# Feed forward's second layer in column blocks of 512, and local attention's probabilities normalised on ScalarE

## The chip, the cores and the metric

The kernel runs on one core of a Trainium2 chip. Its time is the device time of one execution in microseconds (us), here as the median of three runs; smaller is better. The core has five engines that run their own queues in order: TensorE (PE, with its weight loads shown apart as PEld), VectorE (DVE), ScalarE (ACT), GpSimd (POOL) and SyncE (SP), which issues most DMAs.

## The reference, cut to what matters

The program computes two transformer blocks on 512 tokens of width 1024, in float32. The change lies in the second block. Its local attention has eight heads of 64 (two groups of keys and values, four heads each), a window of 128, and a sink in the softmax's sum:

```
scores = where(mask, scores + bias, NEG_INF)
m = max(max(scores), sink)
e = exp(scores - m)
denom = sum(e) + exp(sink - m)
probs = e / denom
out = probs @ v
```

The feed forward is two matrix products, with 4096 hidden features, and a layer norm behind it:

```
ff = square(relu(h @ w_ff1)) @ w_ff2          # 512x1024 @ 1024x4096, then 512x4096 @ 4096x1024
h  = layer_norm(ALPHA * h + ff, ln2_g, ln2_b)
```

## The kernel before, in words

Matrix products keep float32's precision by splitting each operand into a rounded high part and a low part: `mm3` (L94 to L99) multiplies high by high, high by low and low by high into one PSUM bank. `wblock` loads a block of weights of 1 MB by SP's queue into one of two raw slots, and `wsplit` (L77 to L90) makes the high part on ScalarE (L88) and the low part on VectorE (L89), in two halves of 128x1024 each, into one of two high and two low slots. Tokens lie in four tiles of 128 (`NT` = 4).

**Local attention** is `swa_units(c, qT)`, run four times (rounds 0 to 3, c = 0 to 3), each time with two heads, one of each group g, and four blocks n of 128 queries. Each round is interleaved with another generator: round 0 with `u_units(1)` (projections for the pooling mixer), round 1 with `q_units(1)`, round 2 with `u_units(0)`, round 3 with `wo2A_units` (first half of the output projection). In a round, the scores of block n go through L1165 (PE), L1167 and L1169 (VectorE: bias, row maximum). `soft(n)` takes the exponentials on ScalarE with the sums of rows (L1184), adds the sink's term and inverts (L1186, L1187 on VectorE), and multiplies by the inverse on GpSimd (L1189). `mix(n)` transposes the probabilities on PE (L1197), copies them out of PSUM on VectorE for odd n (L1199) and on ScalarE for even n (L1201), and multiplies by the values on PE (L1205). `pool_group` beside it copies a projection on ScalarE (L1222), sums windows on VectorE (L1226, L1229, L1231 gives `dT`), multiplies on PE (L1234) and evicts on ScalarE (L1235) and VectorE (L1236).

**Feed forward** runs in two halves hf of 2048 hidden features. The first layer makes 16 slabs of 128 features by 512 tokens (`fh` and `fl`, high and low), each with 24 matmuls of 512 columns: weights are the stationary operand and the tokens move. In the second layer the slabs are stationary and the weights move: a column block of 256 outputs has four accumulators (one per token tile, two banks "mm" and two banks "sc"), filled from two weight blocks kg of 8 slabs each; `done(t)` adds an accumulator to x1 (L1421). The last column block of the second half runs tile by tile, so that the layer norm can follow.

The order in each engine's queue is set by a scheduler from the program's order and dependencies; a row that waits holds back all behind it on its engine.

Of the kernel before, what the change touches and what calls it, by code (L numbers as in the profile page):

```python
# [13 lines left out]
AF = mybir.ActivationFunctionType  # L14
ALU = mybir.AluOpType
# [13 lines left out]
def hybrid_moe_block(ctx: ExitStack, tc: tile.TileContext, A, out):  # L29
    nc = tc.nc  # L30
    V, P, T, G = nc.vector, nc.scalar, nc.tensor, nc.gpsimd
# [26 lines left out]
    def bank(tag, shape=(128, 512)):  # L58
        return psp.tile(list(shape), F32, name=f"ps_{tag}", tag=tag, bufs=NPS[tag])
# [32 lines left out]
    def wblock(parts, nk=8, n=256, **kw):  # L92
        return wsplit(wload(parts, nk, n), nk, n, **kw)

    def mm3(ps, lh, ll, rh, rl, first=True, last=True):

        seq = list(zip(lh, rh)) + list(zip(lh, rl)) + list(zip(ll, rh))
        for i, (a, b) in enumerate(seq):
            T.matmul(ps, a, b, start=first and i == 0, stop=last and i == len(seq) - 1)  # L99
# [807 lines left out]
    for t in range(NT):  # L907
# [21 lines left out]
                    op=ALU.is_equal)  # L929
# [227 lines left out]
    def swa_units(c, qT):  # L1157

        sc = pa.tile([128, NT, 2, 256], F32, name="sc")
        mx = small.tile([128, NT, 2], F32, name="wmx")  # L1160
        for n in range(NT):
            j0 = 0 if n else 128
            ps = bank("sc", (128, 2, 256))
            for g in range(2):
                T.matmul(ps[:, g, j0:], qT[:, n * 128:(n + 1) * 128], kT[g][:, (n - 1) * 128 + j0:(n + 1) * 128],  # L1165
                         start=True, stop=True)
            V.scalar_tensor_tensor(sc[:, n, :, j0:], ps[:, :, j0:], 0.125, bias[:, c, :, j0:],  # L1167
                                   op0=ALU.mult, op1=ALU.add)
            V.tensor_reduce(mx[:, n], sc[:, n, :, j0:], axis=AX.X, op=ALU.max)  # L1169
            yield  # L1170
        sk = sink[:, None, :, c].to_broadcast([128, NT, 2])
        V.tensor_tensor(mx, mx, sk, op=ALU.max)
        nm = small.tile([128, NT, 2], F32, name="wnm")
        V.tensor_scalar(nm, mx, -1.0, None, op0=ALU.mult)
        es_ = small.tile([128, NT, 2], F32, name="wes")
        V.tensor_tensor(es_, nm, sk, op=ALU.add)
        P.activation(es_, es_, AF.Exp)
        sm = small.tile([128, NT, 2], F32, name="wsm")
        rr = small.tile([128, NT, 2], F32, name="wrr")
        po = bank("po", (128, NT, 128))  # L1180
        def soft(n):
            j0 = 0 if n else 128
            for g in range(2):
                P.activation(sc[:, n, g, j0:], sc[:, n, g, j0:], AF.Exp, bias=nm[:, n, g:g + 1],  # L1184
                             accum_out=sm[:, n, g:g + 1])
            V.tensor_tensor(rr[:, n], sm[:, n], es_[:, n], op=ALU.add)  # L1186
            V.reciprocal(rr[:, n], rr[:, n])  # L1187
            scn = sc[:, n, :, j0:]
            G.tensor_tensor(scn, scn, rr[:, n, :, None].to_broadcast([128, 2, 256 - j0]), op=ALU.mult)  # L1189

        def mix(n):
            nj = 2 if n else 1
            pt = bank("pt", (128, 2, 2, 128))
            eT = pa.tile([128, 2, 2, 128], F32, name="eT")
            for g in range(2):
                for j in range(2 - nj, 2):
                    T.transpose(pt[:, g, j], sc[:, n, g, j * 128:(j + 1) * 128], ident)  # L1197
            if n % 2:
                V.tensor_copy(eT[:, :, 2 - nj:], pt[:, :, 2 - nj:])  # L1199
            else:  # L1200
                P.activation(eT[:, :, 2 - nj:], pt[:, :, 2 - nj:], AF.Copy)  # L1201
            for j in range(2 - nj, 2):
                for g in range(2):
                    gs = slice(64 * g, 64 * g + 64)
                    T.matmul(po[gs, n], vv[:, n - 1 + j, gs], eT[:, g, j], start=j == 2 - nj, stop=j == 1,  # L1205
                             skip_group_check=True)

        soft(0)
        yield
        for n in range(NT):  # L1210
            if n < NT - 1:
                soft(n + 1)
            mix(n)
            yield
        pof = po.rearrange("p a b -> p (a b)")
        P.activation(yTh[1][:, c], pof, AF.Copy)
        V.tensor_tensor(yTl[1][:, c], pof, yTh[1].bitcast(F32)[:, c], op=ALU.subtract)
        yield
# [79 lines left out]
    ALPHA = 2.0 ** 0.25  # L1298
# [51 lines left out]
    gr, br = row("ln1_g_2"), row("ln1_b_2")  # L1350
# [14 lines left out]

    w_ff1 = A["w_ff1_2"].rearrange("o (k p) n -> p (o k) n", p=128)
    w_pg = A["w_ple_gate_2"].rearrange("o (k p) n -> p (o k) n", p=128)
    w_ff2 = A["w_ff2_2"].rearrange("o (g k p) n -> p (o g) k n", p=128, k=8)
    es7.close()
    es8 = ExitStack()  # L1370
    pw = es8.enter_context(tc.tile_pool(name="pw", bufs=1, reuse_waits="tile"))
# [3 lines left out]
    for hf in range(2):  # L1375
        qs = [pf.tile([128, 4, S], F32R, name=f"fq{i}", bufs=1) for i in range(3)] + [quad(FR[6 + i]) for i in range(5)]
        fh = [qs[2 * (i // 4)][:, i % 4] for i in range(16)]
# [9 lines left out]
        for b in range(8):  # L1387
            c0 = 2048 * hf + 256 * b
# [13 lines left out]
                ff1_out(2 * b + c, feat3(w, 128 * c))  # L1402
        if hf == 1:
            gr, br = row("ln2_g_2"), row("ln2_b_2")
        for nb in range(4):
            cs = slice(256 * nb, 256 * nb + 256)
            last = hf == 1 and nb == 3
            pss = [bank("mm"), bank("mm"), bank("sc"), bank("sc")]
            ws = {}

            def ff2(t, kg):
                hi, lo = ws[kg]
                ts = slice(t * 128, (t + 1) * 128)
                mm3(pss[t][:, :256], [fh[8 * kg + k][:, ts] for k in range(8)], [fl[8 * kg + k][:, ts] for k in range(8)],
                    [hi[:, k, :256] for k in range(8)], [lo[:, k, :256] for k in range(8)],
                    first=kg == 0, last=kg == 1)

            def done(t):
                xs = x1[:, t, cs]
                if hf == 0:  # L1420
                    V.scalar_tensor_tensor(xs, xs, ALPHA, pss[t][:, :256], op0=ALU.mult, op1=ALU.add)  # L1421
                else:
                    V.scalar_tensor_tensor(xs, pss[t][:, :256], 1.0, xs, op0=ALU.mult, op1=ALU.add,
                                           accum_out=acc[:, t, nb:nb + 1])

            for kg in range(2):
                ws[kg] = wblock([(w_ff2[:, 2 * hf + kg, :, cs], 256)])
                if not last:
                    for t in range(NT):
                        ff2(t, kg)  # L1430
            if last:
                dst = [pw.tile([128, 2048], F32R, name=f"wg{i}") for i in range(2)]
                wg = {0: wblock([(w_pg[:, :, :256], 256)], dst=dst)}
            for t in range(NT):
                if last:
                    ff2(t, 0)
                    ff2(t, 1)
                done(t)
                if last:
                    layer_norm(t, gr, br, 4)  # L1440
                    if t > 1:
                        turn(x1[:, t - 2], t - 2, h_h, h_l)

# [50 lines left out]
```

## Time and profile before

| what | us |
|---|---|
| median of three runs | 1415.14 (1410.7 to 1417.24) |
| the profiled execution, its own time | 1417.58 |
| its span, first to last instruction | 1415.8 |
| TensorE busy | 1327.5 (94%) |
| VectorE, ScalarE, GpSimd busy | 633.8, 407.4, 54.5 |
| local attention with what runs beside it, and the output projection behind it | 870 to 1018 |
| second layer of feed forward, first half | 1085.43 to 1177.45 |
| second layer, second half, first three column blocks | 1267.39 to 1336.40 |

Times in the trace count from the span's start. In a row of the timeline the figures are start and length, then engine, line, operation, output<-input and the count of instructions merged; in brackets stands how long the engine sat idle before it and what released it. Lengths of matmuls include their drain, so a stretch's time is read from one start to the next.

### The profile page before, as it was taken

The page shows a single profiled execution, that of the slowest core. Times are in us where ns is not written, and L with a number is a line of the kernel's source. Part 1 is how long each engine was busy: PE and PEld are TensorE (multiplying, and loading weights), DVE is VectorE, ACT ScalarE, POOL GpSimd, SP SyncE. Part 2 cuts the span into 40 slices and gives each one's busy share as a digit, 9 for nine tenths or more (in the row PEclk, how much of TensorE's full clock was granted, in tenths as well). Part 3 has the DMA queues.
Part 4 walks back from the last instruction along what each step waited for, and adds up shares of the span by engine and source line. Part 5 has one row for each costly group of instructions (what it writes and reads, how often), then busy time and mean ns, then how long its engine had stood idle before and what let it go on. Part 6 is the DMA issues. An engine that isn't in the chain of part 4 may idle for free. (4 is left out here: it accounts for less than half of the span.)

```text
span 1415.8 us, 20242 instructions
## 1 busy us (share of the span) xinstructions
PE 1327.5 (94%) x8025; PEld 970.9 (69%) x8025; DVE 633.8 (45%) x1637; ACT 407.4 (29%) x809; POOL 54.5 (4%) x67
## 2 busy tenths in 40 slices
PE   8999999998998799999768989999999999999998
PEld 8878787885453344444213348677988998889998
DVE  7775538856432031314001145567743224442384
ACT  5445635432121010101001022533433113331231
POOL 0220200200000000000000000210000000000000
PEclk9999999998999999999999999999999999999999
DMA  5211231675789999998999971113322222332331
GB/s 184 91 30 61 58 106 54 212 282 199 306 322 391 419 418 421 418 392 333 413 420 420 420 266 60 52 39 119 119 89 90 90 90 90 95 106 96 122 109 57
DMA packets 107104, 285.11 MB, mean 201 GB/s; under 512 B 6275, under 2 KB 76505, under 8 KB 82430
## 3 DMA queue, kind: packets, MB, share of 16 engines
q1 hardware_dynamic: 101132, 272.85, 51.2%
q10 hardware_dynamic: 4754, 7.09, 1.5%
q0 software_dynamic: 1120, 3.84, 0.8%
q8 instruction: 64, 1.05, 0.3%
q14 instruction: 34, 0.28, 0.1%
HBM read 279.56 MB, written 4.20 MB: 200 GB/s over the span
## 5 line engine op out<-in xcount | busy, mean ns | idle before, releaser
L848 PE MATMUL ps_mm<-slot,xT 128*64 128x512 f32 (+1 forms) x1024 | 211.0, 615 | 28.7 <-DMA slot<-in_w_up_dram 18.8
L89 DVE TENSOR_TENSOR slot<-slot,slot 128x1024 fp32r<-128x1024 f32 (+2 forms) x118 | 141.0, 1210 | 138.9 <-ACT slot L88 87.6
L88 ACT ACTIVATE slot<-slot 128x1024 fp32r<-128x1024 f32 (+2 forms) x126 | 126.0, 1039 | 174.7 <-PE ps_sc L99 105.3
L848 PEld LDWEIGHTS ps_mm<-slot,xT 128*64 128x64 f32 (+1 forms) x1024 | 56.9, 126 | 158.5 <-issue 105.5
L99 PE MATMUL ps_mm<-slot,slot 128*128 128x256 f32 (+1 forms) x976 | 157.6, 314 | 0.1
L99 PE MATMUL ps_mm<-h_h,slot 128*128 128x512 f32 (+1 forms) x640 | 152.6, 387 | 0.0
L99 PEld LDWEIGHTS ps_mm<-slot,slot 128*128 128x128 f32 x976 | 134.7, 190 | 10.1 <-issue 1.0
L99 PEld LDWEIGHTS ps_mm<-h_h,slot 128*128 128x128 f32 x640 | 116.1, 188 | 26.9 <-issue 1.3
L868 PE MATMUL ps_mm<-slot,zz 128*64 128x512 f32 (+1 forms) x512 | 108.5, 605 | 6.7 <-ACT zz L861 4.2
L99 PE MATMUL ps_mm<-slot,hTh 128*128 128x256 f32 (+1 forms) x640 | 94.7, 293 | 1.5 <-DVE ms L178 0.7
L99 PEld LDWEIGHTS ps_mm<-slot,hTh 128*128 128x128 f32 x640 | 83.1, 192 | 8.9 <-issue 5.8
L855 DVE TENSOR_TENSOR zz<-zz,ps_mm 128x512 f32<-128x512 f32 x12 | 8.2, 686 | 159.1 <-PE ps_mm L848 159.1
L99 PE MATMUL ps_mm<-h_l,slot 128*128 128x512 f32 (+1 forms) x320 | 77.9, 385 | 0.0
L868 PEld LDWEIGHTS ps_mm<-slot,zz 128*64 128x64 f32 (+1 forms) x512 | 32.2, 124 | 65.1 <-issue 51.2
L99 PEld LDWEIGHTS ps_mm<-h_l,slot 128*128 128x128 f32 x320 | 58.4, 188 | 13.2
L99 PE MATMUL ps_sc<-slot,slot 128*128 128x256 f32 x448 | 57.5, 283 | 0.0
L99 PEld LDWEIGHTS ps_sc<-slot,slot 128*128 128x128 f32 x448 | 55.3, 191 | 0.0
L887 DVE TENSOR_TENSOR x<-ps_sc,x 128x512 f32<-128x512 f32 x48 | 32.5, 688 | 34.4 <-PE ps_sc L884 34.4
L99 PE MATMUL ps_mm<-slot,hTl 128*128 128x256 f32 (+1 forms) x320 | 46.4, 284 | 0.0
L854 ACT ACTIVATE zz<-ps_mm 128x512 f32<-128x512 f32 x12 | 7.2, 597 | 136.0 <-PE ps_mm L848 136.0
L775 PE MATMUL ps_pt<-ohp,h2h 128*128 128x256 f32 x160 | 40.4, 291 | 4.3 <-ACT xT L764 3.8
L99 PEld LDWEIGHTS ps_mm<-slot,hTl 128*128 128x128 f32 x320 | 41.5, 188 | 0.0
(373 smaller groups left out, 1876.9 us busy)
## 6 DMA issues: line engine op xcount, KB each, us to landing
slot<-in_w_gate_dram SPq DMA_DIRECT2D x64, 1024.0 KB
slot<-in_w_up_dram SPq DMA_DIRECT2D x64, 1024.0 KB
slot<-in_w_down_dram SPq DMA_DIRECT2D x64, 1024.0 KB
slot<-in_w_ff_dram SPq DMA_DIRECT2D x32, 1024.0 KB
slot<-in_w_in_dram SPq DMA_DIRECT2D x12, 1024.0 KB
slot<-in_w_in_dram SPq DMA_DIRECT2D x12, 512.0 KB
slot<-in_w_out_dram SPq DMA_DIRECT2D x8, 512.0 KB
slot<-in_w_ple_gate_dram SPq DMA_DIRECT2D x4, 1024.0 KB
```

The source lines that it names most:

```text
L88: P.activation(h_, r_, AF.Copy)
L89: (eng or V).tensor_tensor(l_, r_, h_.bitcast(F32), op=ALU.subtract)
L99: T.matmul(ps, a, b, start=first and i == 0, stop=last and i == len(seq) - 1)
L775: T.matmul(ps[:, c], hh[:, t, ds_], oh_[:, t, :n], start=i == 0 and t == 0 and (c == 0 or not by_tile), stop=i == 1 and t == NT - 1, skip_ ...
L848: T.matmul(ps[w * e:w * e + w], xT[:, 4 * kh + k, c0 + w * e:c0 + w * e + w], wsrc(m, kh, e, k), start=kh == 0 and k == 0, stop=kh == 1 an ...
L854: P.activation(sl[:n], gu[0][:n], AF.Silu)
L855: V.tensor_tensor(sl[:n], sl[:n], gu[1][:n], op=ALU.mult)
L868: T.matmul(pss[nh][w * e:w * e + w], hT[:, k, w * e:w * e + w], wsrc(2, nh, e, k), start=k == 0, stop=k == 3, skip_group_check=True)
L887: V.tensor_tensor(xs, pc, xs, op=ALU.add)
```

## The change

Two edits. The normalisation in `soft(n)` was one GpSimd operation over both heads; it is two ScalarE copies, one per head, with the inverse as per-partition scale. The second layer of the feed forward takes column blocks of 512 (half 0: two; half 1: one, then two of 256 as before); a weight block of 1 MB is then 4 slabs by 512 columns, so a block of columns has four of them instead of two. The layer norm behind it sums three partial sums instead of four.

```diff
             V.tensor_tensor(rr[:, n], sm[:, n], es_[:, n], op=ALU.add)
             V.reciprocal(rr[:, n], rr[:, n])
-            scn = sc[:, n, :, j0:]
-            G.tensor_tensor(scn, scn, rr[:, n, :, None].to_broadcast([128, 2, 256 - j0]), op=ALU.mult)
+            for g in range(2):
+                scn = sc[:, n, g, j0:]
+                P.activation(scn, scn, AF.Copy, scale=rr[:, n, g:g + 1])
...
-    w_ff2 = A["w_ff2_2"].rearrange("o (g k p) n -> p (o g) k n", p=128, k=8)
+    w_ff2 = A["w_ff2_2"].rearrange("o (k p) n -> p (o k) n", p=128)
...
-        for nb in range(4):
-            cs = slice(256 * nb, 256 * nb + 256)
-            last = hf == 1 and nb == 3
+        blocks = [(0, 512), (512, 512)] if hf == 0 else [(0, 512), (512, 256), (768, 256)]
+        for nb, (c0, nc_) in enumerate(blocks):
+            cs = slice(c0, c0 + nc_)
+            last = hf == 1 and nb == 2
             pss = [bank("mm"), bank("mm"), bank("sc"), bank("sc")]
+            nk = 2048 // nc_
+            NK = 16 // nk
...
-                mm3(pss[t][:, :256], [fh[8 * kg + k][:, ts] for k in range(8)], [fl[8 * kg + k][:, ts] for k in range(8)],
-                    [hi[:, k, :256] for k in range(8)], [lo[:, k, :256] for k in range(8)],
-                    first=kg == 0, last=kg == 1)
+                mm3(pss[t][:, :nc_], [fh[nk * kg + k][:, ts] for k in range(nk)], [fl[nk * kg + k][:, ts] for k in range(nk)],
+                    [hi[:, k] for k in range(nk)], [lo[:, k] for k in range(nk)], first=kg == 0, last=kg == NK - 1)
...
-            for kg in range(2):
-                ws[kg] = wblock([(w_ff2[:, 2 * hf + kg, :, cs], 256)])
+            for kg in range(NK):
+                k0 = 16 * hf + nk * kg
+                ws[kg] = wblock([(w_ff2[:, k0:k0 + nk, cs], nc_)], nk=nk, n=nc_)
...
-                    layer_norm(t, gr, br, 4)
+                    layer_norm(t, gr, br, 3)
```

The scheduler moves instructions with it. ScalarE's queue in round 0 before, from the table load at the first exponential (`wnm` minus the row maximum, `wsm` the sums, `pad` the pooling projection, `eT` transposed probabilities, `slot_7754` the high part of the weight block that PE takes up at the end of round 1):

```order
L1184 ACT_TABLE_LOAD
L1184 ACTIVATE sc,wsm<-sc,wnm 128x128
L1177 ACTIVATE wes<-wes 128x8
L1184 ACTIVATE sc,wsm<-sc,wnm 128x128
L1184 ACTIVATE sc,wsm<-sc,wnm 128x256 x3
L1222 ACTIVATE pad_7145<-ps_mm 128x512
L1201 ACTIVATE eT<-ps_pt 128x2x128
L1184 ACTIVATE sc,wsm<-sc,wnm 128x256 x3
L88 ACTIVATE slot_7754<-slot_7752 128x1024 x2
L1201 ACTIVATE eT<-ps_pt 128x512
```

The same place of ScalarE's queue with the change (L1190 is the new copy, `wrr` the inverse; lines behind it are one higher, so L1223 is the former L1222):

```order
L1184 ACTIVATE sc,wsm<-sc,wnm 128x256
L1190 ACTIVATE sc<-sc,wrr 128x128 x2
L1184 ACTIVATE sc,wsm<-sc,wnm 128x256
L1223 ACTIVATE pad_7145<-ps_mm 128x512
L1190 ACTIVATE sc<-sc,wrr 128x256 x2
L1202 ACTIVATE eT<-ps_pt 128x2x128
L1184 ACTIVATE sc,wsm<-sc,wnm 128x256 x4
L88 ACTIVATE slot_7762<-slot_7760 128x1024 x2
L1190 ACTIVATE sc<-sc,wrr 128x256 x4
L1236 ACTIVATE slot_7134<-ps_mm,cols 128x512
L1202 ACTIVATE eT<-ps_pt 128x512
```

The copies of block 1 stand behind the copy of `pad`, and those of blocks 2 and 3 behind both halves of a weight split.

PE's queue in round 0 before, from the second product with the values to the first projections of round 1:

```order
L1205 MATMUL ps_po<-eT,vv 64x128 x4
L1197 MATMUL ps_pt<-ident,sc 128x128 x8
L1234 MATMUL ps_mm<-dT,wp 128x512
L99 MATMUL ps_mm<-h_h,slot_7599 128x512 x8
L99 MATMUL ps_mm<-h_l,slot_7599 128x512 x8
```

There one L1205 stood on each side of L1234, and both ahead of L99. With the change:

```order
L1206 MATMUL ps_po<-eT,vv 64x128 x4
L1235 MATMUL ps_mm<-dT,wp 128x512
L1198 MATMUL ps_pt<-ident,sc 128x128 x8
L99 MATMUL ps_mm<-h_h,slot_7603 128x512 x2
L99 MATMUL ps_mm<-h_h,slot_7603 128x512 x5
```

The pooling product now stands ahead of the transposes of blocks 2 and 3, and seven projection matmuls ahead of the last product with the values (one L1206 follows the two, one the five).

PE's queue at the start of the second layer before (`slot_9080` high and `slot_9081` low weights, `fq_8426` and `fq_8428` high slabs, `fq_8427` low):

```order
L99 MATMUL ps_mm<-slot_9080,fq_8426 128x256 x4
L99 MATMUL ps_mm<-slot_9080,fq_8428 128x256 x4
L99 MATMUL ps_mm<-slot_9081,fq_8426 128x256 x4
L99 MATMUL ps_mm<-slot_9081,fq_8428 128x256 x4
L99 MATMUL ps_mm<-slot_9080,fq_8427 128x256 x4
L99 MATMUL ps_mm<-slot_9080,slot_8429 128x256 x4
```

And with the change, where these rows are one token tile's share of one weight block:

```order
L99 MATMUL ps_mm<-slot_9096,fq_8442 128x512 x4
L99 MATMUL ps_mm<-slot_9097,fq_8442 128x512 x4
L99 MATMUL ps_mm<-slot_9096,fq_8443 128x512 x4
L99 MATMUL ps_sc<-slot_9096,fq_8442 128x512 x4
L99 MATMUL ps_sc<-slot_9097,fq_8442 128x512 x4
```

A token tile's share of a weight block goes from 24 matmuls of 256 columns to 12 of 512.

## Rows read from the trace of the kernel before

**Rows 1.** The page's first part: busy time, share of the span, instructions.

```profile
span 1415.8 us, 20242 instructions
PE 1327.5 (94%) x8025; PEld 970.9 (69%) x8025; DVE 633.8 (45%) x1637; ACT 407.4 (29%) x809; POOL 54.5 (4%) x67
```

**Rows 2.** Stretches by stage: length, busy us (instructions) per engine, granted clock, DMA, GB/s.

```profile
870.00:1018.00 148.00, 141.58 (x804) 112.81 (x803) 101.72 (x218) 59.25 (x132) 16.48 (x16) 0.99 0.25 74
...
1085.43:1177.45 92.02, 92.02 (x770) 92.01 (x769) 26.04 (x33) 15.56 (x17) 0.00 (x0) 1.00 0.29 93
1177.45:1267.39 89.94, 89.94 (x386) 72.32 (x385) 38.77 (x47) 35.64 (x48) 0.00 (x0) 1.00 0.30 94
1267.39:1336.40 69.01, 69.01 (x578) 69.00 (x577) 21.42 (x38) 13.55 (x15) 0.00 (x0) 1.00 0.28 92
```

**Rows 3.** Timeline of ScalarE and VectorE around the second layer's second column block.

```profile
1097.13 2.01 ACT L88 ACTIVATE slot<-slot 128x1024 fp32r<-128x1024 f32 x2 [8.60 <-PE ps_sc L99]
...
1098.23 2.36 DVE L89 TENSOR_TENSOR slot<-slot,slot 128x1024 fp32r<-128x1024 f32 x2 [8.62 <-ACT slot L88]
...
1108.66 0.42 DVE L1421 SCALAR_TENSOR_TENSOR x<-x,ps_sc 128x256 f32<-128x256 f32 x1 [2.46 <-PE ps_sc L99]
```

**Rows 4.** VectorE groups by form: an accumulator of 512 columns added to x1.

```profile
L1310 DVE SCALAR_TENSOR_TENSOR x<-x,ps_mm 128x512 f32<-128x512 f32 x8 | 5.5, 683 | 9.3 <-PE ps_mm L99 9.3
```

**Rows 5.** PE's timeline in local attention, its waits and the end of round 0.

```profile
894.99 0.66 PE L1197 MATMUL ps_pt<-ident,sc 128*128 128x128 f32 x4 [1.57 <-POOL sc L1189]
895.99 0.66 PE L1197 MATMUL ps_pt<-ident,sc 128*128 128x128 f32 x4 [0.34 <-POOL sc L1189]
...
897.61 2.08 PE L1234 MATMUL ps_mm<-dT,wp 128*128 128x512 f32 x2
...
900.39 2.13 PE L99 MATMUL ps_mm<-h_h,slot 128*128 128x512 f32 x8
...
933.23 0.55 PE L1197 MATMUL ps_pt<-ident,sc 128*128 128x128 f32 x3 [0.40 <-POOL sc L1189]
...
936.91 0.44 PE L1197 MATMUL ps_pt<-ident,sc 128*128 128x128 f32 x2 [0.61 <-POOL sc L1189]
...
961.64 0.66 PE L1205 MATMUL ps_po<-eT,vv 128*64 128x128 f32 x8 [0.84 <-DVE eT L1199]
```

**Rows 6.** Stretches of one us in round 0, columns as in rows 2.

```profile
897.00:898.00 1.00, 1.00 (x9) 0.67 (x6) 1.00 (x3) 0.00 (x0) 0.00 (x0) 0.50 0.00 0
...
899.00:900.00 1.00, 1.00 (x5) 0.38 (x6) 0.10 (x1) 0.28 (x1) 0.00 (x0) 0.50 0.00 0
```

**Rows 7.** ScalarE groups by form in local attention: busy us, mean ns, idle before.

```profile
L1184 ACT ACTIVATE sc<-sc,wnm 128x256 f32<-128x256 f32 x24 | 11.9, 498 | 0.0
...
L1184 ACT ACTIVATE sc<-sc,wnm 128x128 f32<-128x128 f32 x8 | 3.2, 395 | 13.7 <-DVE wnm L1174 13.6
...
L1201 ACT ACTIVATE eT<-ps_pt 128x256 f32<-128x256 f32 x4 | 1.5, 373 | 0.0
```

**Rows 8.** ScalarE's timeline in round 0, the last exponentials and what follows.

```profile
890.76 0.51 ACT L1184 ACTIVATE sc<-sc,wnm 128x256 f32<-128x256 f32 x1
891.16 0.20 ACT L1184 ACTIVATION_READ_ACCUMULATOR sc<-sc,wnm 128x1 f32 x1
...
891.75 1.99 ACT L88 ACTIVATE slot<-slot 128x1024 fp32r<-128x1024 f32 x2
895.74 0.60 ACT L1201 ACTIVATE eT<-ps_pt 128x512 f32<-128x512 f32 x1 [2.00 <-PE ps_pt L1197]
```

**Rows 9.** GpSimd's normalisation: count, then shortest, median and longest duration in ns.

```profile
L1189 POOL TENSOR_TENSOR sc<-sc,wrr x16: 612/1039/1923, 887.4 to 957.4; 128x512 f32<-128x512 f32 x12, 128x256 f32<-128x256 f32 x4
```

**Rows 10.** VectorE's timeline beside GpSimd's operations, rounds 0 and 3.

```profile
895.49 0.99 DVE L1231 SCALAR_TENSOR_TENSOR dT<-pad,pad 128x512 f32<-128x512 f32 x1
...
954.61 1.03 DVE L1186 TENSOR_TENSOR wrr<-wsm,wes 128x2 f32<-128x2 f32 x1 [0.18 <-ACT sc L1184]
...
957.18 3.21 DVE L89 TENSOR_TENSOR slot<-slot,slot 128x1024 fp32r<-128x1024 f32 x2
```

More of the change, by code (lines that the diff above doesn't have):

```diff
@@ L1420, in done @@
                 if hf == 0:
-                    V.scalar_tensor_tensor(xs, xs, ALPHA, pss[t][:, :256], op0=ALU.mult, op1=ALU.add)
+                    V.scalar_tensor_tensor(xs, xs, ALPHA, pss[t][:, :nc_], op0=ALU.mult, op1=ALU.add)
                 else:
-                    V.scalar_tensor_tensor(xs, pss[t][:, :256], 1.0, xs, op0=ALU.mult, op1=ALU.add,
+                    V.scalar_tensor_tensor(xs, pss[t][:, :nc_], 1.0, xs, op0=ALU.mult, op1=ALU.add,
                                            accum_out=acc[:, t, nb:nb + 1])
-            for kg in range(2):
-                ws[kg] = wblock([(w_ff2[:, 2 * hf + kg, :, cs], 256)])
+            for kg in range(NK):
+                k0 = 16 * hf + nk * kg
+                ws[kg] = wblock([(w_ff2[:, k0:k0 + nk, cs], nc_)], nk=nk, n=nc_)
                 if not last:
```

## The prediction

> **What bounds the kernel now.** I read the busy shares first: TensorE works 94% of the span, ScalarE 29% and VectorE 45% [rows 1], so the question in each stage is whether TensorE has gaps and what a matmul costs where it has none. Next the stretches by stage [rows 2]. In both halves of the feed forward's second layer TensorE is busy for the whole stretch (92.02 of 92.02 us, 69.01 of 69.01 us) at the full granted clock: only the price per matmul can move the end there. In local attention with the output projection it is busy 141.58 of 148.00 us; 6.4 us are gaps. Third, the timeline of TensorE in that stretch [rows 5] says who closes the gaps: four of those shown end with GpSimd's normalisation (1.57, 0.34, 0.40 and 0.61 us) and one with VectorE's copy of transposed probabilities (0.84 us). So each of the two edits touches something that ends a wait or is the bound itself.
>
> **Second layer of the feed forward.** A column block of 256 has 2 weight blocks x 4 token tiles x 24 = 192 matmuls; half 0 has four of them, 768 matmuls in 92.02 us, so 0.1198 us each; the 576 of half 1 take 69.01 us, 0.1198 us again [rows 2]. The price of 512 columns I take from the first layer of half 1: 16 slabs x 24 = 384 matmuls in 89.94 us, 0.2342 us each, also without a gap [rows 2]. Two matmuls of 256 cost 0.2396 us, one of 512 costs 0.2342: 5.4 ns less per pair. Half 0 turns its 768 into 384 of 512: 384 x 0.2342 = 89.94 us, so -2.08 us. Half 1 turns 384 of its 768 (two of four blocks) into 192: -1.04 us. Sum -3.1 us. The 192 of the last block, which runs by token tile, stay as they are and only come earlier.
>
> The first layer has the weights stationary and the tokens moving, the second layer the other way round. If wide moving weights came no cheaper per column, the gain would be 0; that is one end, and -3.1 us the other. I take -3.1, because the 256-column row of the second layer [rows 2] already moves weights without any gap, so nothing but the fixed part per matmul should differ.
>
> What must stay hidden there: a weight block is 2048 columns per partition as before, one token tile's share is 12 x 0.2342 = 2.81 us instead of 24 x 0.1198 = 2.88, and a whole block lasts 11.24 instead of 11.5 us. The split of the block after next starts when its high slot is free, at 1097.13, and VectorE ends it at 1098.23 + 2.36 = 1100.6 us, about 8 us before TensorE comes to it [rows 3]. That cover shrinks by 0.26 us and not more. DMA moves 93 GB/s at a share of 0.29 [rows 2] and the same bytes as before, so a load has room as well. An accumulator of 512 columns goes to x1 in 0.68 us [rows 4] instead of 0.42 [rows 3], but in half as many operations, and the bank is wanted again at the earliest two tiles later (5.6 us): nothing waits. The sum of three partials instead of four in the layer norm is one instruction of the same kind; I cost it at nothing, as the tile before it covers it.
>
> The Trainium skill ("TensorE: Matmul & The Clock Gate", section "Back-to-back issue gap") gives a warm matmul N columns at 2.4 GHz plus about 2.5 ns, that is 109.2 ns for 256 and 215.8 ns for 512. By it the edit would save 576 x 2.6 ns = 1.5 us, half of what the rows give; the rows stand at 119.8 and 234.2 ns, above both, and I keep to them.
>
> **Normalisation on ScalarE.** Removed: 16 GpSimd operations, median 1.04 us [rows 9]. Added: 24 ScalarE copies of 128x256 and 8 of 128x128. The trace has no such copy with a scale from SBUF. Nearest is the exponential on the same tile: it takes 0.498 and 0.395 us [rows 7], but the next instruction starts after 0.40 us (890.76 to 891.16) [rows 8], and by the same 0.10 of overlap after 0.30 for 128 columns. So 24 x 0.40 + 8 x 0.30 = 12.0 us more on ScalarE, 3.0 us a round. Bounds: the plain copy of 256 columns, 0.373 us [rows 7] less the same overlap, would make it some 8 us, the full durations 15 us. In a stretch of 148 us where ScalarE works 59 [rows 2] the load fits; what counts is the order, since ScalarE's queue is now held by copies that wait for VectorE's inverse, and copies are held by whatever stands ahead.
>
> Round 0: before, GpSimd let TensorE transpose blocks 2 and 3 at 894.99 and 895.99 [rows 5]. Now copies of blocks 0 and 1 (2 x 0.30 + 2 x 0.40 = 1.4 us) come ahead of the weight split that began at 891.75 and lasts 2.0 us [rows 8]; it ends at about 895.1, and the copies of blocks 2 and 3 at about 895.9 and 896.7, 0.8 to 1.0 us later than GpSimd's results. But in the new order TensorE does the pooling product in that wait. Its input `dT` was written by 895.49 + 0.99 = 896.5 us, and 0.3 us of that operation were lost beside GpSimd [rows 10] (another VectorE operation of 128x512 takes 0.68 [rows 4]); I expect it at about 895.7. Then come the transposes to about 898.3, then the products with the values, which wait for `eT` and between which seven projection matmuls (1.6 us of work) now stand; they end at about 901.4 with 41 of the 48 projections left, where before at 900.39 [rows 5] all 48 were left. 901.4 - 1.6 = 899.8: -0.6 us.
>
> Round 1 has a full TensorE before (its projections run from 900.39 on). ScalarE comes 3 us later to the second copy of queries and to `eT` of block 0; three projections (0.7 us) moved ahead of its reader cover most: I take +0.4 us. Round 2 is like round 0, but the copies of block 2 stand behind the split, and the eviction of the pooling product between them: the transposes wait to about 938.5 where GpSimd released them at 936.91 [rows 5], with the pooling product and two matmuls moved into the wait: +0.5 us. In round 3 the new order computes the last scores before the second-to-last round's end, some 6 us earlier, and VectorE's weight split is no longer drawn out (3.21 us for what takes 2.36 elsewhere [rows 3, 10]): the 0.84 us wait on `eT` [rows 5] goes, -0.8 us. Sum -0.5 us. Everything behind local attention runs without a gap up to the last column block, so the sum reaches the end.
>
> **Sum.** -3.1 - 0.5 = -3.6 us. The profiled execution took 1417.58 us, 1.8 more than its span, and would come to 1414.0. It is 2.4 us above the median of 1415.14, and from the median the forecast is **1411.5 us**.
>
> **Rivals.**
>
> *VectorE and GpSimd stop blocking each other, and all of attention's stalls go.* For it: an addition of two columns took 1.03 us beside GpSimd [rows 10], and GpSimd's longest operation 1.92 against a median of 1.04 [rows 9]. If the five gaps (3.76 us) vanish [rows 5], TensorE may also keep its clock: after the first two gaps the granted clock stood at 0.50 (1.2 GHz) from 897 to 900 [rows 6], some 3 us of busy time at half speed, 1.5 us lost. That gives -3.1 - 5.3 = -8.4 us, 1406.7. Against it: the new copies come later in rounds 0 and 2. The Trainium skill ("SBUF — State Buffer", section "SBUF: two separate sides") says that VectorE and GpSimd share a port pair as an exclusive lock while ScalarE has its own, which is this mechanism; the stretched rows agree.
>
> *ScalarE's queue becomes the bound of rounds 0 and 2.* There each exponential waits behind a copy that waits for an inverse on VectorE, and no projections lie beside it. If the 3.0 us a round are wholly exposed (6.0 us) and the longer gap in round 2 costs the clock once more (1.5 us), the sum is 7.5 - 3.1 = +4.4 us, 1419.5: slower than before. It decides from 3.1 us of added gap in the two rounds together. Against it: the moved pooling product and projections.
>
> *The wide blocks do not do what they say:* 512 moving weight columns cost twice 256, or the last slabs of the first layer come late. Then only attention's -0.5 us is left, 1414.6. For it speaks only that the trace has no such row in this stage.
>
> **How the numbers follow.** Forecast 0.62 (its own range 1409 to 1414); VectorE freed 0.15; ScalarE the bound 0.10; no gain from wide blocks 0.13. About 0.5% (7.1 us) is what a measurement of this kernel can tell from no change, so faster means below 1408.1 and slower above 1422.2. Only the first rival reaches the one, in a little over half its cases, and the second the other at the worst end of its ScalarE price: faster 0.08, same 0.89, slower 0.03. The runs shown differ by 6.5 us, so a median moves by a few us by itself. The range runs from 1407 (nearly all of the first rival) to 1417.5 (half of the second).
>
> **What would show it.** Right: the stretch of the second layer in half 0 lasts about 89.9 us and the three blocks of half 1 about 68.0, without a gap and with about 0.234 us from one wide matmul to the next; GpSimd has no row in local attention and no two-column addition takes as long as 1.03 us; the first projections of the feed forward start within 2 us of where they did. Wrong: a gap of TensorE at the start of a wide block; gaps of 2 us and more in rounds 0 or 2 that ScalarE ends; a second stretch of granted clock 0.50.

## The result, and the profile after

The changed kernel took 1410.22 us (median of 14 runs, 1403.22 to 1418.75), the kernel before, on the same chip, 1417.63 us (14 runs, 1410.7 to 1422.75): a ratio of 0.9947, 95% interval 0.9930 to 0.9964. That is 7.4 us less, where the forecast was 3.6, and 3.6 of 1417 us (0.9975) lies outside the interval. The direction was right, the size was half of what came. The time itself lies only 1.3 us below the forecast 1411.5, and that is luck: the kernel before measured 2.5 us above the median that the forecast started from, and the gain was 3.8 us larger. The first lines of the page of after (its profiled run took 1405.39 us) answer to [rows 1]:

```profile
span 1403.6 us, 19075 instructions
...
PE 1320.1 (94%) x7449; PEld 939.6 (67%) x7449; DVE 627.6 (45%) x1621; ACT 419.8 (30%) x841; POOL 38.0 (3%) x51
```

The spans of the two profiled runs differ by 12.2 us, more than the medians, so the time has to be read stage by stage, from one start to the next. These are windows of after that answer to [rows 2]: attention (from its first score matmul to the first 512-column matmul of feed forward), second layer of half 0, first layer of half 1, first blocks of the second layer in half 1.

```profile
865.63:1011.27 145.64, 140.70 (x802) 112.70 (x800) 97.38 (x218) 71.21 (x164) 0.00 (x0) 0.99 0.25 75
...
1078.74:1167.05 88.31, 88.31 (x385) 72.07 (x384) 24.72 (x25) 15.56 (x17) 0.00 (x0) 1.00 0.29 96
1167.05:1257.01 89.96, 89.96 (x385) 72.33 (x384) 39.03 (x47) 35.65 (x48) 0.00 (x0) 1.00 0.30 94
1257.01:1324.20 67.19, 67.19 (x386) 59.05 (x384) 20.96 (x30) 13.55 (x15) 0.00 (x0) 1.00 0.29 94
```

The same stretch of attention before, in a window cut at the same instructions:

```profile
870.51:1017.96 147.45, 141.03 (x801) 112.39 (x800) 101.68 (x218) 58.70 (x132) 16.48 (x16) 0.99 0.25 74
```

| stage | before | after | measured | forecast |
|---|---|---|---|---|
| all up to attention's first score (same code) | 870.51 | 865.63 | -4.9 | 0 |
| attention and output projection | 147.45 | 145.64 | -1.8 | -0.5 |
| second layer, half 0 | 92.02 | 88.31 | -3.7 | -2.08 |
| first layer, half 1 (same code) | 89.94 | 89.96 | 0.0 | 0 |
| second layer, half 1, first blocks | 69.01 | 67.19 | -1.8 | -1.04 |

The first row is no part of the change: in the eleven profiled runs of this study, whose edits lie behind it but for one fill of a tile with ones, it ended anywhere from 865.6 to 874.4 us. The three changed stages sum to -7.3 us, which is what the medians say. TensorE has no gap in the second layer, so its gain is the price of the wide matmul. By weight block of 48 matmuls, in the first column block of half 0 of after:

```profile
1078.74:1089.95 11.21, 11.21 (x50) 9.01 (x49) 3.56 (x4) 1.50 (x3) 0.00 (x0) 1.00 0.28 94
1089.95:1101.12 11.17, 11.17 (x49) 9.01 (x48) 2.36 (x2) 2.01 (x2) 0.00 (x0) 1.00 0.27 95
1101.12:1112.03 10.91, 10.91 (x50) 9.01 (x48) 2.36 (x2) 2.01 (x2) 0.00 (x0) 1.00 0.27 96
1112.03:1122.92 10.89, 10.89 (x50) 9.01 (x48) 4.33 (x5) 2.01 (x2) 0.00 (x0) 1.00 0.29 98
```

The reader sees two prices at the same clock, with the same load beside them: 11.2 / 48 = 0.233 us in blocks 0 and 1, 10.9 / 48 = 0.227 in blocks 2 and 3; mean 0.2300, where the forecast had 0.2342. The second column block has the same pattern.

In attention, TensorE's timeline of after answers to [rows 5]. All its waits above 0.15 us between round 0's transposes and round 3's end are these, and one of 0.29 us that both kernels have:

```profile
887.76 0.66 PE L1206 MATMUL ps_po<-eT,vv 128*64 128x128 f32 x8 [0.26 <-DVE eT L1200]
890.51 1.12 PE L1235 MATMUL ps_mm<-dT,wp 128*128 128x512 f32 x2 [2.09 <-DVE dT L1232]
...
931.62 1.13 PE L1235 MATMUL ps_mm<-dT,wp 128*128 128x512 f32 x2 [0.25 <-DVE dT L1232]
```

Before there were 1.57, 0.34, 0.40, 0.61 and 0.84 us [rows 5], and one of 0.44 in round 0. So no transpose waits for a normalisation any more; TensorE waits for the pooling mixer's `dT` instead. The stretch at half clock of [rows 6] stayed, now from about 892 to 895 us. ScalarE's copies by form answer to [rows 7]. Behind them stands VectorE's two-column addition in local attention, first before, then after; the 1.03 us of [rows 10] was one of the 16.

```profile
L1190 ACT ACTIVATE sc<-sc,wrr 128x256 f32<-128x256 f32 x24 | 10.8, 498 | 0.1
L1190 ACT ACTIVATE sc<-sc,wrr 128x128 f32<-128x128 f32 x8 | 2.8, 393 | 0.0
```

```profile
L1186 DVE TENSOR_TENSOR wrr<-wsm,wes 128x2 f32<-128x2 f32 x16 | 4.8, 301 | 7.5 <-ACT sc L1184 7.5
```

```profile
L1186 DVE TENSOR_TENSOR wrr<-wsm,wes 128x2 f32<-128x2 f32 x16 | 2.4, 156 | 10.7 <-ACT sc L1184 10.7
```

### The profile page after: what moved, and what is told of

The parts are those of the page before. It is cut to its first block, busy times and chain, and to the rows that moved or that the text cites. A ratio compares the mean times of both kernels' runs of the same rounds, so it can differ in the third digit from the quotient of the medians.

```text
span 1403.6 us, 19075 instructions
## 1 busy us (share of the span) xinstructions
PE 1320.1 (94%) x7449; PEld 939.6 (67%) x7449; DVE 627.6 (45%) x1621; ACT 419.8 (30%) x841; POOL 38.0 (3%) x51
## 5 line engine op out<-in xcount | busy, mean ns | idle before, releaser
L848 PE MATMUL ps_mm<-slot,xT 128*64 128x512 f32 (+1 forms) x1024 | 213.9, 628 | 26.6 <-DMA slot<-in_w_up_dram 17.2
L89 DVE TENSOR_TENSOR slot<-slot,slot 128x1024 fp32r<-128x1024 f32 (+2 forms) x118 | 140.1, 1202 | 160.1 <-ACT slot L88 106.3
L99 PE MATMUL ps_mm<-slot,slot 128*128 128x256 f32 (+1 forms) x808 | 155.4, 343 | 0.2
L99 PE MATMUL ps_mm<-h_h,slot 128*128 128x512 f32 (+1 forms) x640 | 153.7, 388 | 0.0
L99 PEld LDWEIGHTS ps_mm<-slot,slot 128*128 128x128 f32 x808 | 124.7, 190 | 17.3 <-issue 1.5
L99 PEld LDWEIGHTS ps_mm<-h_h,slot 128*128 128x128 f32 x640 | 116.4, 189 | 26.9 <-issue 1.5
L99 PE MATMUL ps_mm<-slot,hTh 128*128 128x256 f32 (+1 forms) x640 | 93.8, 291 | 1.8 <-DVE ms L178 0.8
L99 PEld LDWEIGHTS ps_mm<-slot,hTh 128*128 128x128 f32 x640 | 82.2, 190 | 9.1 <-issue 5.8
L99 PE MATMUL ps_mm<-h_l,slot 128*128 128x512 f32 (+1 forms) x320 | 78.2, 385 | 0.0
L99 PEld LDWEIGHTS ps_mm<-h_l,slot 128*128 128x128 f32 x320 | 58.3, 188 | 13.3 <-issue 0.2
L99 PE MATMUL ps_sc<-slot,slot 128*128 128x512 f32 (+1 forms) x280 | 54.4, 347 | 0.0
L99 PEld LDWEIGHTS ps_sc<-slot,slot 128*128 128x128 f32 x280 | 45.3, 189 | 6.7
L99 PE MATMUL ps_mm<-slot,hTl 128*128 128x256 f32 (+1 forms) x320 | 46.4, 284 | 0.0
L99 PEld LDWEIGHTS ps_mm<-slot,hTl 128*128 128x128 f32 x320 | 41.5, 188 | 0.0
```

Source lines behind the costliest of these rows:

```text
L89: (eng or V).tensor_tensor(l_, r_, h_.bitcast(F32), op=ALU.subtract)
L848: T.matmul(ps[w * e:w * e + w], xT[:, 4 * kh + k, c0 + w * e:c0 + w * e + w], wsrc(m, kh, e, k), start=kh == 0 and k == 0, stop=kh == 1 an ...
```

## The experiments

The two layers of feed forward repeat to 0.1 us between profiles of kernels that share their code, so one profile tells a few tenths of a us there; the medians do not. Of the kernels below, the two with one edit alone and the last two were timed several times; the five between them ran once and are read by their windows.

**Each edit alone.** The first kernel keeps the wide blocks and has GpSimd's line back (the diff is against after); the second is the kernel before with the reverse of it.

```diff
+            scn = sc[:, n, :, j0:]
+            G.tensor_tensor(scn, scn, rr[:, n, :, None].to_broadcast([128, 2, 256 - j0]), op=ALU.mult)
-            for g in range(2):
-                scn = sc[:, n, g, j0:]
-                P.activation(scn, scn, AF.Copy, scale=rr[:, n, g:g + 1])
```

> Only the wide column blocks of the second layer; attention's normalisation stays on GpSimd. Theory A (the wide matmul is cheaper than forecast, 0.2300 us on average instead of 0.2342, and the two edits add up): the stretch from the first to the last second-layer matmul of half 0 takes 88.3 us against 92.0 before, and the first two column blocks of half 1 67.2 against 69.0, so this kernel is 5.5 us (0.39%) faster than before. Theory B (the forecast's price of 0.2342 us holds and the rest of the gain came with attention's edit, for instance by other buffers' addresses): 3.1 us (0.22%) faster, with blocks of half 0 near 89.9 us. Attention to the first matmul of feed forward: 122.7 us as before by both.

> Only attention's normalisation on ScalarE; the second layer in blocks of 256 as before. Theory A (gain by stage as the trace of after shows): attention to the first matmul of feed forward 120.9 us against 122.7, the kernel 1.8 us (0.13%) faster. Forecast: 0.5 us faster (122.2). Rival (ScalarE's queue becomes the bound in rounds 0 and 2): 4.4 us slower, 127.1. The second layer: 92.0 and 69.0 us as before by all.

The windows of attention and of the second layer in half 0, of the first kernel and then of the second:

```profile
870.60:1018.10 147.50, 141.07 (x802) 112.41 (x800) 101.68 (x218) 58.70 (x132) 16.47 (x16) 0.99 0.25 74
1085.57:1173.88 88.31, 88.31 (x385) 72.08 (x384) 24.72 (x25) 15.56 (x17) 0.00 (x0) 1.00 0.30 96
```

```profile
870.08:1015.69 145.61, 140.68 (x802) 112.72 (x800) 97.42 (x218) 71.21 (x164) 0.00 (x0) 0.99 0.26 75
1083.15:1175.14 91.99, 91.99 (x769) 91.99 (x768) 26.04 (x33) 15.55 (x17) 0.00 (x0) 1.00 0.29 92
```

To 0.05 us, the stage with the edit comes out as in after and the other as before: the edits are independent and add up, theory A in both cases. (The 122.7 and 120.9 us of the expectations end at the first matmul of feed forward, which has 256 columns; there the traces have 122.8 and 120.9.) By time the first kernel is at 0.9973 (0.9952 to 0.9994) and the second at 0.9978 (0.9957 to 0.9999) of the kernel before; the first interval holds 5.5 us but also 3.1, the second 1.8 but also 0.5, so it is the windows that decide.

**What sets the price of a wide matmul.** In after the four weight blocks differ in where the stationary slabs lie. Two kernels separate place from order: one lists the slabs of the weight slots first and those of the pool `fq` last, the other takes the weight blocks in the order 3, 2, 1, 0.

```diff
-        qs = [pf.tile(..., name=f"fq{i}", bufs=1) for i in range(3)] + [quad(FR[6 + i]) for i in range(5)]
+        qs = [quad(FR[6 + i]) for i in range(5)] + [pf.tile(..., name=f"fq{i}", bufs=1) for i in range(3)]
```

```diff
-            for kg in range(NK):
+            for kg in (range(NK - 1, -1, -1) if NK > 2 else range(NK)):
```

> After, with the hidden activations' slabs in another order: the five that lie in the weight slots first, the three of the pool fq last. In after the 48 wide matmuls of weight blocks 0 and 1 took 11.2 us (0.233 each) and those of blocks 2 and 3 10.9 (0.227). Theory L (price depends on where the stationary slab lies; fq0 to fq2 and the slab in FR[6] are the dear places, FR[7] to FR[10] the cheap ones): block 1, now in FR[8] and FR[9], falls to 10.9 us, block 3, now in fq1 and fq2, rises to 11.2; block 2, mixed, lies between. Theory P (price depends on the position in the accumulation, or on the data and what runs beside it): 11.2, 11.2, 10.9, 10.9 as in after.

> After, with the four weight blocks of each wide column block taken in the order 3, 2, 1, 0 (same sums, added in another order). Theory L (place of the stationary slab): in order of time 10.9, 10.9, 11.2, 11.2 us. Theory P (position in the accumulation, the banks' first writes or what runs beside it): 11.2, 11.2, 10.9, 10.9 in order of time, as in after.

Windows of the four weight blocks, in order of time, with other slabs:

```profile
1079.81:1090.69 10.88, 10.88 (x49) 9.01 (x48) 3.56 (x4) 1.49 (x3) 0.00 (x0) 1.00 0.30 96
1090.69:1101.57 10.88, 10.88 (x49) 9.01 (x48) 2.36 (x2) 2.01 (x2) 0.00 (x0) 1.00 0.31 98
1101.57:1112.68 11.11, 11.11 (x50) 9.01 (x48) 2.36 (x2) 2.01 (x2) 0.00 (x0) 1.00 0.31 94
1112.68:1123.87 11.19, 11.19 (x49) 9.01 (x48) 4.34 (x5) 2.01 (x2) 0.00 (x0) 1.00 0.26 95
```

and in reversed order (the second column block):

```profile
1124.54:1135.46 10.92, 10.92 (x49) 9.01 (x48) 3.05 (x3) 2.01 (x2) 0.00 (x0) 1.00 0.31 96
1135.46:1146.35 10.89, 10.89 (x49) 9.01 (x48) 2.36 (x2) 2.01 (x2) 0.00 (x0) 1.00 0.34 97
1146.35:1157.53 11.18, 11.18 (x49) 9.01 (x48) 2.36 (x2) 2.01 (x2) 0.00 (x0) 1.00 0.31 95
1157.53:1168.73 11.20, 11.20 (x50) 9.01 (x48) 4.33 (x5) 2.01 (x2) 0.00 (x0) 1.00 0.31 94
```

The price goes with the place, and the position in the accumulation has no part in it. One detail of theory L fell: the slab in FR[6], which it counted among the dear places, is cheap here (block 0 of the first kernel). That left which property of the place decides. The built program gives the tiles' byte addresses in a partition: `fq0` to `fq2` 89,216 to 113,792; `h_h` and `h_l` 23,680 to 56,448; all weight slots 137,440 to 229,344. So every cheap block had moving and stationary tile both high, and every dear one had them mixed: in all of its matmuls (11.2 us), in two thirds (11.17) or in one third (11.11, block 2 of the first kernel). Mixed throughout was also the first layer of feed forward (moving tokens low, stationary weights high), from which the forecast took 0.2342. The next kernel moves weights as well: those of block 0 to 72,832 to 89,216, those of blocks 1 and 3 to 137,440 to 154,336.

```diff
+    cur.update(hi=(FR[6], FR[3]), lo=(FR[8], FR[5])) 
+        qs = [pf.tile(..., name=f"fq{i}", bufs=1) for i in range(3)] + [quad(i) for i in (FR[2], FR[7], FR[4], FR[9], FR[10])]
+                low = [pw.tile([128, 2048], F32R, name=f"wg{i}") for i in range(2)] if nc_ == 512 and kg == 0 else None
-                ws[kg] = wblock([(w_ff2[:, k0:k0 + nk, cs], nc_)], nk=nk, n=nc_)
+                ws[kg] = wblock([(w_ff2[:, k0:k0 + nk, cs], nc_)], nk=nk, n=nc_, dst=low)
```

> After, with other places in SBUF for the wide second-layer blocks: weight block 0 has moving weights and stationary slabs both at low addresses (73 to 106 thousand bytes), block 1 has moving weights at 137 to 154 thousand and its stationary slab fq2 at 106 to 114 thousand, blocks 2 and 3 both at high addresses. In after blocks 0 and 1 were mixed and far apart (low slab, moving at 171 to 229 thousand): 11.2 us for 48. Theory H (cheap when moving and stationary lie in the same half of the partition, dear when one is below and one above about 131 thousand): 10.9, 11.2, 10.9, 10.9. Theory D (dear when they lie far apart): 10.9, 10.9, 10.9, 10.9. Theory U (cheap only where both lie high): 11.2, 11.2, 10.9, 10.9.

Blocks 0 to 2 of its first column block, and blocks 0 and 1 of the second:

```profile
1089.44:1100.36 10.92, 10.92 (x49) 9.01 (x48) 3.56 (x4) 1.49 (x3) 0.00 (x0) 1.00 0.28 97
1100.36:1111.54 11.18, 11.18 (x49) 9.01 (x48) 2.36 (x2) 2.01 (x2) 0.00 (x0) 1.00 0.31 95
1111.54:1122.44 10.90, 10.90 (x49) 9.01 (x48) 2.36 (x2) 2.01 (x2) 0.00 (x0) 1.00 0.30 96
...
1133.34:1144.26 10.92, 10.92 (x50) 9.01 (x48) 3.05 (x3) 2.01 (x2) 0.00 (x0) 1.00 0.30 97
1144.26:1155.43 11.17, 11.17 (x49) 9.02 (x48) 0.00 (x0) 0.00 (x0) 0.00 (x0) 1.00 0.00 0
```

Theory H: both low is cheap, mixed is dear even where the tiles are 24 thousand bytes apart, so neither distance nor a cheap upper half is the rule. The last row excludes what runs beside it: VectorE, ScalarE and DMA are idle there, and the price is the dear one. (This kernel's time, 1415.24 us in one run, isn't used: its stretch of attention ran from 870.27 to 1021.98, 151.7 us, with a wait of TensorE of 3.39 us for VectorE (L1342) at the output projection and a granted clock of 0.50 from 988 to 994.)

**Attention: what did the edit give, and what do the copies cost?** One kernel adds a GpSimd product of the removed one's shape and inputs' timing, on tiles that nobody reads; one leaves the normalisation out.

```diff
+            du = pa.tile([128, 2, 256], F32, name="du", bufs=2)
+            G.tensor_tensor(du[:, :, j0:], dsrc[:, :, j0:], rr[:, n, :, None].to_broadcast([128, 2, 256 - j0]), op=ALU.mult)
```

```diff
-            for g in range(2):
-                scn = sc[:, n, g, j0:]
-                P.activation(scn, scn, AF.Copy, scale=rr[:, n, g:g + 1])
```

> After, with a GpSimd product of the same shape and start as the removed one added back on tiles that nobody reads (ScalarE still normalises). Theory S (what attention gained is that VectorE no longer stands beside GpSimd's tensor operation): VectorE's reciprocals L1186 again reach about 1 us beside it, the splits L89 again 3 us in places, and the stretch from attention's first score matmul to the first 512-column matmul of feed forward goes from 145.6 us (as in after, with the half-clock stretch in round 0; about 144.1 without it) most of the way back to 147.5. Theory Q (what it gained is the shorter way from reciprocal to transpose, GpSimd's queue and its 0.6 to 1.9 us per product): 145.6 (144.1) as in after.

> After, without the normalisation (attention's probabilities go unnormalised into the transposes, so its output is not the reference's). It prices ScalarE's 32 copies. Theory: they are nearly all beside other work, the same stretch falls from 145.6 us (144.1 without the half-clock stretch) by 0 to 0.6 us. Rival: they sit on the path of the transposes, 4 tokens blocks a round at about 0.8 us in the two rounds with little filler, then it falls by 2 us or more.

The stretch with the added product, and then TensorE's two waits for `dT` in it (line numbers are four higher):

```profile
874.40:1021.34 146.94, 141.12 (x801) 112.75 (x800) 98.98 (x218) 71.46 (x164) 15.25 (x16) 0.99 0.26 75
```

```profile
899.69 0.70 PE L1239 MATMUL ps_mm<-dT,wp 128*128 128x512 f32 x1 [2.50 <-DVE dT L1236]
...
941.63 1.13 PE L1239 MATMUL ps_mm<-dT,wp 128*128 128x512 f32 x2 [0.69 <-DVE dT L1236]
```

1.3 of the 1.8 us come back (both runs had the half clock): 0.85 as longer waits for `dT` (2.50 and 0.69 against 2.09 and 0.25 us), the rest in TensorE's busy time (141.12 against 140.70 us), for which the runs show no cause. The trace shows where the waits come from. In round 0 VectorE's operation that writes `dT` runs beside two of the added products and takes 1.08 us, where it takes 0.68 in after:

```profile
898.05 2.49 POOL L1194 TENSOR_TENSOR du<-dsrc,wrr 128x512 f32<-128x512 f32 x2 [4.14 <-DVE pad L1234]
898.55 1.08 DVE L1236 SCALAR_TENSOR_TENSOR dT<-pad,pad 128x512 f32<-128x512 f32 x1
```

In round 2 it is a window sum ahead of `dT` (1.50 us from 936.93, 0.69 in after). So theory S has the larger part, by the operations that lead to `dT`. Of those that it named, one split L89 is drawn out, to 1.46 us where it takes 1.22 elsewhere, and the two-column additions stay short: none of the 16 runs beside an added product.

```profile
L1188 DVE TENSOR_TENSOR wrr<-wsm,wes 128x2 f32<-128x2 f32 x16 | 2.4, 156 | 10.6 <-ACT sc L1186 10.6
```

Without the normalisation (no stretch at half clock) attention takes:

```profile
874.31:1016.04 141.73, 138.73 (x802) 111.70 (x800) 97.97 (x218) 58.66 (x132) 0.00 (x0) 1.00 0.26 77
```

The like runs of after's attention code are the two kernels on slabs, which also escaped the half clock; the first of them:

```profile
868.22:1012.34 144.12, 139.18 (x801) 111.56 (x800) 97.40 (x218) 71.14 (x164) 0.00 (x0) 1.00 0.25 76
```

So the copies cost 144.12 - 141.73 = 2.4 us, not 0 to 0.6: the rival was right in size. Its way, the transposes, is not what the trace shows. Without the copies TensorE's wait for `dT` in round 2 is gone, and that in round 0 is 0.80 us instead of 2.09:

```profile
899.92 0.70 PE L1232 MATMUL ps_mm<-dT,wp 128*128 128x512 f32 x1 [0.80 <-DVE dT L1229]
```

**A version that beats both.** Theory H says that the first layer pays the dear price throughout. This kernel puts its weights low, beside the tokens; the slabs go high, all but one.

```diff
+    def low(i):
+        return [(pf if i else pw).tile([128, 2048], F32R, name=("wl" if i else "wg") + str(j), bufs=1) for j in range(2)]
+    def high():
+        return [slot(FR[2], F32R), slot(FR[4], F32R)]
+        qs = [pf.tile([128, 4, S], F32R, name="fq0", bufs=1)] + [quad(FR[i]) for i in (6, 7, 8, 9, 10, 3, 5)]
-            w = wblock([(w_ff1[:, :, c0:c0 + 256], 256)])
+            w = wblock([(w_ff1[:, :, c0:c0 + 256], 256)], dst=low(b % 2) if hf or b > 1 else None)
-                ws[kg] = wblock([(w_ff2[:, k0:k0 + nk, cs], nc_)], nk=nk, n=nc_)
+                dst = high() if kg % 2 else low(1 if last else kg // 2)
+                ws[kg] = wblock([(w_ff2[:, k0:k0 + nk, cs], nc_)], nk=nk, n=nc_, dst=dst)
```

> After, with the first layer's weights (all blocks but the first two of half 0) at low addresses, beside h_h and h_l; in the second layer one slab and weight blocks 0 and 2 low, blocks 1 and 3 high with high slabs. Theory H (a 512-column matmul of this pair form costs 0.2267 us when moving and stationary tile lie on the same side of some address between 114 and 137 thousand, 0.233 to 0.234 when not): first layer of half 1 falls from 89.96 us by 384 x 0.0075 = 2.9 to 87.1, that of half 0 (first 512-column matmul to the second layer) from 67.47 by 288 x 0.0075 = 2.2 to 65.3; in the second layer block 0 has 8 of 12 on one side, 1 and 3 all, 2 none, so half 0 about 88.2; the kernel 5.2 us (0.37%) below after, some 12.5 (0.9%) below before. If the first layer stays at 89.96, the rule does not hold for the moving activations and the kernel is as after.

First layer of half 0 from its first 512-column matmul, second layer of half 0, first layer of half 1:

```profile
1014.22:1079.54 65.32, 65.32 (x291) 54.07 (x290) 29.93 (x37) 27.55 (x38) 0.00 (x0) 1.00 0.30 97
1079.54:1167.78 88.24, 88.24 (x385) 72.14 (x384) 24.71 (x25) 15.77 (x17) 0.00 (x0) 1.00 0.31 96
1167.78:1254.86 87.08, 87.08 (x385) 72.07 (x384) 38.96 (x47) 35.23 (x48) 0.00 (x0) 1.00 0.31 97
```

All three came out as expected (65.3, 88.2, 87.1). It took 1403.15 us (median of 6) against 1417.85 for the kernel before: a ratio of 0.9901 (0.9866 to 0.9936; the two medians by themselves give 0.9896). The last kernel adds attention's normalisation on VectorE.

```diff
-                P.activation(scn, scn, AF.Copy, scale=rr[:, n, g:g + 1])
+                V.tensor_scalar(scn, scn, rr[:, n, g:g + 1], None, op0=ALU.mult)
```

> As the run before it, and attention's normalisation on VectorE (tensor_scalar) in place of ScalarE. Leaving the copies out gave attention 2.4 us; theory: what it costs is the copies' place behind two weight splits L88 and the exponentials in ScalarE's queue, VectorE has room, and 1 us or more of the 2.4 comes back (attention's stretch 143.1 or less without the half-clock stretch, 144.6 with it). Rival: on VectorE the 32 products of some 0.3 us stand before the chain to dT and the gap of 2.1 us at dT grows by as much as the transposes gain: 144.1 (145.6) or more.

```profile
871.35:1014.86 143.51, 139.95 (x801) 111.89 (x800) 108.44 (x252) 59.85 (x133) 0.00 (x0) 1.00 0.30 89
```

Without the half clock it is 143.51 against 144.12: 0.6 us, so the stretch missed the 143.1 that the theory had set. But that stretch ends with feed forward's first matmuls of 256 columns, which take longer in the last two kernels: from the last turning of x (L186 at 986.67) on 28.19 us here and 28.05 in the kernel before it, against 27.69 in the kernel on slabs. Up to there, slabs first, then this kernel:

```profile
868.22:984.65 116.43, 111.49 (x577) 84.50 (x575) 74.71 (x173) 57.59 (x144) 0.00 (x0) 1.00 0.24 73
871.35:986.67 115.32, 111.99 (x576) 84.67 (x575) 83.64 (x205) 45.06 (x112) 0.00 (x0) 1.00 0.24 74
```

That is 1.1 us, what the theory had said of attention, and the rival failed: the wait for `dT` in round 0 did not grow but fell from 2.09 us to 0.16, while a new one of 0.76 stands before the transposes.

```profile
895.62 1.12 PE L1235 MATMUL ps_mm<-dT,wp 128*128 128x512 f32 x2 [0.16 <-DVE dT L1232]
```

By time the last kernel is at 0.9883 (0.9856 to 0.9911) of the kernel before, not to be told from the run before it. Neither was timed against the change itself. By their traces both beat it: from attention's first score to the end the change takes 538.0 us, the first of the two 533.2, the last 530.8. Of the last difference some 1.5 us are the granted clock, which did not fall there.

## Why the prediction was right in sign and half in size

- **The price of a wide matmul is the term that was mis-sized.** "The price of 512 columns I take from the first layer" gave 0.2342 us, with the reason that "nothing but the fixed part per matmul should differ". The first layer is a case of mixed sides; in the second layer half of the weight blocks have both tiles on one side at 0.2267. At the mean of 0.2300 the pair saves 9.6 ns instead of 5.4: 576 x 9.6 ns = 5.5 us, as measured (3.71 + 1.82). The estimate by the formula of the Trainium skill ("TensorE: Matmul & The Clock Gate", section "Back-to-back issue gap"), which that section calls the gap of an isolated matmul, 215.8 ns and so 1.5 us, was further off: no block of 48 comes below 226.7 ns each.
- **What must stay hidden there** stayed hidden: TensorE is busy 88.31 of 88.31 us.
- **The sum in attention was too small** (-0.5 against -1.8). Round 0 was forecast at -0.6 and gave about nothing in waits: 1.57 + 0.34 + 0.44 us went, 2.09 + 0.26 came. `dT` was there as forecast (wait ended 24.9 us after the first score, forecast 25.2), but the stretch at half clock came on top again. (The copies of blocks 2 and 3 at 895.9 and 896.7 would be 0.9 and 0.7 us behind GpSimd's results, not 0.8 to 1.0; the sum does not use it.) Rounds 1 to 3 were forecast at +0.1; the waits of 0.40, 0.61 and 0.84 us went and one of 0.25 came, -1.6. Round 3 came as forecast (-0.8). The steps that failed are round 1, forecast at +0.4, where TensorE waits in neither kernel, and above all round 2, forecast at +0.5 and measured at -0.40 - 0.61 + 0.25 = -0.76. There "the transposes wait to about 938.5" was right as a time (67.4 us after the first score, forecast 68.0), but not as a wait: the pooling product, four more scores and matmuls of the output projection filled it.
- **ScalarE's price** was right: the copies take 0.498 and 0.393 us, as long as the exponentials of [rows 7], and ScalarE's busy time in the stretch rose by 12.5 us (58.70 to 71.21), forecast 12.0.
- **Rivals.** That VectorE and GpSimd block each other holds in part: 1.3 of 1.8 us came back with a GpSimd product beside it. But the stall of round 0 changed hands rather than went, and the clock still fell. ScalarE's queue as the bound of rounds 0 and 2 is real as a cost (2.4 us), but below what GpSimd had cost, so no loss. The wide blocks do what they say. Of the signs of being wrong, a gap of over 2 us in round 0 did come, ended by VectorE's `dT` and not by ScalarE.

## What to carry to other kernels

A price taken from another stage holds only if the operands lie alike, not just the shape: compare where both tiles lie before a per-matmul price is carried over. When an edit shortens one producer's way, list who is late next in the same in-order queue (here `dT`), and sum waits that go against waits that come. Where unchanged code scatters by several us between runs, read a small change from windows cut at the same instructions.

## What the runs showed of the hardware that was not expected

- Back-to-back float32r matmuls of 128x512 take 0.2267 to 0.2279 us each, by block, when moving and stationary tile lie on the same side of an address between 118 and 137 thousand bytes of the partition (low-low and high-high alike; the highest low tile, weights of the last two kernels, ends at 117,888, the lowest high one starts at 137,440). They take 0.2331 to 0.2343 when all of a block lie on different sides. Where in between the border is was not tried. For 256 columns no such difference shows: in the kernel before a block of 96 mixed in 20 of 24 and the next, both high, take 11.5 us each:

```profile
1131.44:1142.93 11.49, 11.49 (x99) 11.49 (x98) 2.78 (x3) 2.01 (x2) 0.00 (x0) 1.00 0.28 93
1142.93:1154.44 11.51, 11.51 (x98) 11.51 (x97) 3.53 (x5) 2.01 (x2) 0.00 (x0) 1.00 0.31 93
```

- Within a block the rule is not exact. In block 1 of after four matmuls with both tiles high stand behind eight mixed ones, and take 0.93 us from start to start, the dear price:

```profile
1091.81 1.10 PE L99 MATMUL ps_mm<-slot,slot 128*128 128x512 f32 x4
1092.74 2.02 PE L99 MATMUL ps_mm<-slot,fq 128*128 128x512 f32 x8
```

  In block 2 of the kernel with other slabs eight both high stand behind four mixed, and take 1.85 us, 0.231 each:

```profile
1104.33 2.02 PE L99 MATMUL ps_mm<-slot,slot 128*128 128x512 f32 x8
1106.18 1.09 PE L99 MATMUL ps_mm<-slot,fq 128*128 128x512 f32 x4
```

  So same-side matmuls right behind mixed ones are dearer too, and a block with a third mixed took anywhere from 10.99 us (block 0 of the last kernel but one) to 11.11. What passes the price on was not tried; the sums above go by whole blocks.
- The granted clock of [rows 6] is not fixed by the code. Six profiled runs have the same attention code and the same wait of 2.09 us; behind it the clock fell to 0.50 (1.2 GHz) in four of them, after among them, and stayed at 1.00 in the two kernels that separate place from order. Attention took 145.64 us in after and 144.12 with other slabs, so the fall costs 1.5 us. One of the microseconds in each, first after:

```profile
892.63:893.63 1.00, 1.00 (x5) 0.59 (x3) 1.00 (x3) 0.24 (x1) 0.00 (x0) 0.50 0.00 0
```

```profile
895.22:896.22 1.00, 1.00 (x11) 0.55 (x10) 1.00 (x3) 0.22 (x1) 0.00 (x0) 1.00 0.00 0
```

  What decides it stays open.
- A GpSimd product draws out some VectorE operations that run beside it and not others. In the kernel before, a two-column addition of two tiles in SBUF took 1.03 us beside one [rows 10], and the operation that writes `dT` took 1.08 beside the added one. The addition of the bias to the scores (L1169 in that kernel, one input in PSUM), which starts at 899.56 beside the same added products, took 0.68 us, as in after. Which property of the operation decides was not tried.
